# Two-layer hybrid encoder trunk on one core: order of the queues, norms inside the output projections, gain row spread by TensorE

## The chip, the cores and the metric

The kernel runs as one launch on 1 core of one Trainium2 chip. The metric is the device time of that core in microseconds (us). Of the kernel before, 3 runs are given: median 3146.25 us (3145.14 to 3149.17).

## The reference

512 tokens of width 1024 pass through two layers, all in float32:

```
x = x + even_mix(rms_norm(x))   # conformer convolution (GLU, causal conv 31, LayerNorm, swish)
                                # beside chunked gated linear attention; one output projection
x = x + peer_ffn(rms_norm(x))
x = x + fox_mix(rms_norm(x))    # forgetting attention: QK norm, forget gates, causal softmax, out projection
x = x + peer_ffn(rms_norm(x))

def peer_ffn(h):                # 8 heads, 128 x 128 product keys, 16 of 16384 experts for each head
    q = h @ wq; s1, s2 = scores against two key tables
    top 16 of each, 256 sums, top 16 of these -> experts, gates = softmax
    act = gelu(h . u[expert]);  out = sum(gates * act * v[expert])
```

## The kernel before

Tokens are in four blocks of 128 rows. `self.xb[b]` holds block b of x ([128, 1024]); `hT` is the normalised x, turned so that the width lies on the partitions, and kept as two parts, `hhi` (rounded to fp32r) and `hlo` (the rest). A product is made of three fp32r matmuls: hi by hi, hi by lo, lo by hi (`mm3`, L75 to L79). Weights come through `weight` (L54): a DMA from the SP queue into `raw` (4 buffers of 512 KB), then ScalarE makes `whi` (L50) and VectorE, or GpSimd where `eng` says so, makes `wlo` (L51), with 3 buffers each.

The stages follow one another: `mix_even`, `peer(0)`, `mix_odd`, `peer(1)`.

Each stage begins with a norm (`rms_h`, L87 to L125). For a block, `scale` takes the sum of squares (ScalarE, L104, into a tile `sq` of its own), makes the root (VectorE L105, GpSimd L106) and writes `xs` = x times root times gain (VectorE L107); `flip` turns `xs` by 8 transposes (TensorE L114) and splits the result into hi (ScalarE L116) and lo (VectorE L117). The gain row `grow` is loaded by a DMA that repeats it on all 128 partitions (L85, 512 KB).

A mixing part ends in `out_proj` (L194): for each half c of the output columns four accumulators, one for each block, are filled over 4 weight tiles (`kp`, each two k-steps, so 24 matmuls of 512 columns for four blocks). In the second half the last three weight tiles run block after block, in the order 1, 2, 3, 0, and each block is added to x (L199). The norm of the PEER stage is traced behind that.

In the attention (`mix_odd_body`) the scores run in units: (head pair, head, block of queries). `unit()` does the `logits` of one unit (L639 to L648), the `flip` of the unit three back (L658 to L663) and, after a head's last, `values` (L671). `project(hp, w, unit)` calls `unit()` after every second k-step, 56 times in all; 12 calls are left and run ahead of `out_proj` (L704). PSUM tiles come from a pool of 6 banks (`bank`, L72) and one of 2.

`peer_body` (L814): queries and routing of 8 heads, four `u_step`s behind each head (L938). A `u_step` (L842) multiplies one of 128 tiles of u by the tokens of blocks 1 to 3: 24 matmuls of 384 columns, then Gelu. Beside the steps after routing the gate table G is built (`gate4`, L891) and stored to DRAM, and block 0's own expert rows are gathered on the GpSimd queue. When the last gate is built, the pool of the v stage is opened and `fetch` (L950) is called for the first eight places (L1007): it loads parts of G (`gc`, 1.5 MB, L957) and stored activations (`at`, L960) on the SP queue. In the v stage `prepare(n)` (L962) loads a v tile, multiplies `gc` by the activations (L971) and splits the product into `wh` and `wl`; `v_sweep` (L1022) does 18 matmuls of 512 columns for each n.

Each engine and each DMA queue works through a fixed list in order. The program is traced in Python, and a planner puts each engine's instructions in order by times that it simulates, the earlier traced first where several could go. `tc.issue_after(ins)` holds what is traced within it behind `ins` on the same engine or queue.

## Time and profile before

| | us |
|---|---|
| median of 3 runs | 3146.25 |
| profiled execution, own time | 3148.14 |
| its span, first to last instruction | 3146.3 |
| TensorE busy | 3080.9 (98% of the span) |
| VectorE busy | 2406.8 (76%) |
| ScalarE busy | 1437.2 (46%) |
| GpSimd busy | 1155.1 (37%) |

The span is what one core's engines need; the time has the start and end around it. Matmuls overlap one another, so busy time of TensorE is no measure of work, but its idle time and the clock that it was granted can be read place by place.

### The profile page before, as it was taken

To read this page: it belongs to the slowest core of one execution; us is meant where nothing else is said; L and a number is where in the kernel's file an instruction comes from. 1 tells how busy PE (TensorE), PEld (TensorE's weight loads), DVE (VectorE), ACT (ScalarE), POOL (GpSimd) and SP (SyncE) were. 2 spreads that over 40 slices of the span, in tenths; PEclk is the share of its full clock that TensorE was granted. 3 is DMA by queue.
4 is the path that set the end of the run, shared out by engine and by line. 5 is a ranking of instruction groups with operands and counts; after the bars stand their busy time and mean duration, and the time that the engine had idled before them with its cause. 6 is when DMAs were issued, how large, how long until landed. Compare 5 with 4: busy or idle time off the path is not lost.

```text
span 3146.3 us, 45733 instructions
## 1 busy us (share of the span) xinstructions
PE 3080.9 (98%) x15932; PEld 2696.8 (86%) x15932; DVE 2406.8 (76%) x4936; ACT 1437.2 (46%) x2258; POOL 1155.1 (37%) x800
## 2 busy tenths in 40 slices
PE   8999999999999999999999999999999999999999
PEld 6668999999999888877766679999999998888787
DVE  6765998888885888888535548998888867888786
ACT  4343334666664333333356633336666643333332
POOL 1220122996773332332100000227976752233330
PEclk9999999999999999999999999999999999999999
DMA  4113445999998999999421124448999997999996
GB/s 155 54 34 125 137 140 168 358 351 347 339 323 292 310 350 372 352 350 356 148 81 41 41 77 132 137 144 313 375 340 339 339 322 260 354 367 346 355 349 233
DMA packets 334202, 787.16 MB, mean 250 GB/s; under 512 B 26745, under 2 KB 181770, under 8 KB 327826
## 3 DMA queue, kind: packets, MB, share of 16 engines
q1 hardware_dynamic: 260242, 515.76, 47.0%
q0 software_dynamic: 73728, 268.47, 24.1%
q8 instruction: 125, 2.05, 0.3%
q14 instruction: 107, 0.88, 0.1%
HBM read 687.59 MB, written 96.47 MB: 249 GB/s over the span
## 4 chain that ended last, share of the span: by engine, by line
PE 90%; DVE 3%; DMA 2%; issue 1%; ACT 1%; SPq 1%; POOL 1%; DVEq 0%; ACTq 0%; POOLq 0%
PE acc L1027 33%; PE pu L79 10%; PE pu L78 10%; PE pu L77 10%; PE bank L77 5%; PE bank L79 5%; PE bank L78 5%; PE bank L911 5%; PE po L671 1%; PE pc L284 1%; PE bank L639 1%; PE bank L935 1%; DVE wlo L51 1%; SPq L960 1%; POOL gr L861 1%
## 5 line engine op out<-in xcount | busy, mean ns | idle before, releaser
L50 ACT ACTIVATE whi<-raw 128x1024 fp32r<-128x1024 f32 x604 | 636.9, 1057 | 829.5 <-PE pu L78 471.6
L51 DVE TENSOR_TENSOR wlo<-raw,whi 128x1024 fp32r<-128x1024 f32 x565 | 692.1, 1226 | 183.1 <-ACT whi L50 156.3
L77 PE MATMUL pu<-hhi,whi 128*128 128x384 f32 x2048 | 702.0, 343 | 9.6 <-ACT whi L50 8.7
L79 PE MATMUL pu<-hhi,wlo 128*128 128x384 f32 x2048 | 691.0, 338 | 2.2 <-DVE wlo L51 2.2
L78 PE MATMUL pu<-hlo,whi 128*128 128x384 f32 x2048 | 689.2, 337 | 0.0
L872 POOL DMA_INDIRECT gr<-in_vF_dram,ids x256 | 317.7, 1241 | 717.7 <-DVE x L874 658.7
L1027 PE MATMUL acc<-wlo,wh 128*128 128x512 f32 x1536 | 472.7, 389 | 0.0
L1027 PE MATMUL acc<-whi,wl 128*128 128x512 f32 x1536 | 472.5, 389 | 0.0
L1027 PE MATMUL acc<-whi,wh 128*128 128x512 f32 x1536 | 436.5, 390 | 9.3 <-ACT whi L50 9.3
L861 POOL DMA_INDIRECT gr<-in_uN_dram,ids x256 | 352.5, 1377 | 237.6 <-DVE dots L863 140.7
L50 ACT ACTIVATE wh<-gc 128x384 fp32r<-128x384 f32 x256 | 134.4, 525 | 645.7 <-PE acc L1027 638.0
L77 PEld LDWEIGHTS pu<-hhi,whi 128*128 128x128 f32 x2048 | 388.3, 190 | 12.1 <-ACT whi L50 9.3
L79 PEld LDWEIGHTS pu<-hhi,wlo 128*128 128x128 f32 x2048 | 387.3, 189 | 4.0 <-DVE wlo L51 3.9
L78 PEld LDWEIGHTS pu<-hlo,whi 128*128 128x128 f32 x2048 | 388.1, 190 | 1.9 <-DVE hlo L117 0.6
L1027 PEld LDWEIGHTS acc<-whi,wh 128*128 128x128 f32 x1536 | 287.6, 188 | 72.1 <-ACT whi L50 12.6
L1027 PEld LDWEIGHTS acc<-wlo,wh 128*128 128x128 f32 x1536 | 288.3, 188 | 60.0
L1027 PEld LDWEIGHTS acc<-whi,wl 128*128 128x128 f32 x1536 | 288.3, 188 | 59.8
L901 POOL TENSOR_SCALAR a<-cst,sT 128x128 f32<-128x128 f32 x192 | 330.6, 1722 | 13.2 <-PE bank L911 4.9
L874 DVE SCALAR_TENSOR_TENSOR x<-gr,dots,x 128x1024 f32<-128x1024 f32 x256 | 327.4, 1279 | 0.3
L863 DVE CUSTOM_DVE_ANT_0 gr<-gr,h 128x1024 f32<-128x1024 f32 x256 | 307.9, 1221 | 23.8 <-DMA gr<-in_uN_dram,ids 23.7
L51 DVE TENSOR_TENSOR wl<-gc,wh 128x384 fp32r<-128x384 f32 x256 | 142.7, 558 | 179.4 <-ACT wh L50 170.0
L51 POOL TENSOR_TENSOR wlo<-raw,whi 128x1024 fp32r<-128x1024 f32 x39 | 99.0, 2540 | 398.5 <-ACT whi L50 390.5
(248 smaller groups left out, 4242.3 us busy)
## 6 DMA issues: line engine op xcount, KB each, us to landing
raw<-in_uT_dram SPq DMA_DIRECT2D x256, 512.0 KB
raw<-in_vF_dram SPq DMA_DIRECT2D x256, 512.0 KB
G<-big SPq DMA_DIRECT2D x48, 1024.0 KB
gc<-G SPq DMA_DIRECT2D x32, 1536.0 KB
aside<-xact SPq DMA_DIRECT2D x208, 192.0 KB
at<-aside SPq DMA_DIRECT2D x104, 384.0 KB
raw<-in_w_in_dram SPq DMA_DIRECT2D x32, 512.0 KB
raw<-in_wq_dram SPq DMA_DIRECT2D x32, 512.0 KB
```

Source lines behind the costliest of these rows:

```text
L50: first = self.nc.scalar.activation(hi, raw, AF.Copy)
L51: self.last_lo = (eng or self.nc.vector).tensor_tensor(lo, raw, hi.bitcast(F32), op=ALU.subtract)
L77: mm(out, lh, rh, start=first, stop=False)
L78: mm(out, lh, rl, start=False, stop=False)
L79: return mm(out, ll, rh, start=False, stop=last)
L861: nc.gpsimd.indirect_dma_start(out=r, out_offset=None, in_=uN, in_offset=bass.IndirectOffsetOnAxis(ap=ids[:, s:s + 1], axis=0))
L863: return lambda: nc.vector.tensor_tensor_reduce(r, r, h0, 1.0, 0.0, ALU.mult, ALU.add, accum_out=dots[:, s:s + 1])
L872: nc.gpsimd.indirect_dma_start(out=r, out_offset=None, in_=vF, in_offset=bass.IndirectOffsetOnAxis(ap=ids[:, s:s + 1], axis=0))
L874: return lambda: nc.vector.scalar_tensor_tensor(self.x0, r, dots[:, s:s + 1], self.x0, op0=ALU.mult, op1=ALU.add)
L901: (nc.vector if t else nc.gpsimd).tensor_scalar(a1[:, t], self.iota, e1[:, t:t + 1], gate[:, t:t + 1], op0=ALU.is_equal, op1=ALU.mult)
L911: nc.tensor.matmul(p[:, t], a2[:, t], a1[:, t], start=True, stop=True)
L1027: nc.tensor.matmul(acc[b][c], wt[:, s], vt[:, c], start=(n == 0 and wt is wh and vt is vh), stop=(n == NE1 - 1 and wt is wl))
```

## The change

Seven edits, with names that the diff shows:

1. The first gain row is loaded once (4 KB) and spread over 128 partitions by a matmul with a row of ones; then come the loads of x, of four weight tiles (`early`) and of the constants. The table `steps` is loaded and widened in `peer(0)`, by GpSimd.
2. `norm` replaces `rms_h`: its three parts `scale`, `flip`, `close` are called one by one. Sums of squares write into `xs` itself, which has 3 buffers (4 in the first norm).
3. `out_proj` opens the next norm and scales blocks 1, 2 and 3 as they are added (`ends`). `chain` holds the pieces in order on TensorE. In `mix_odd` a new `hT` is there, and the flips of 1, 2 and 3 stand between the pieces of block 0; in `mix_even` they stand behind them, in `peer`.
4. `peer` scales block 0, then one `u_step` is run, then block 0 is flipped; head 0 is followed by three steps and not four.
5. The last 12 units of the attention are called within the first half of `out_proj`, four after each of its weight tiles.
6. The forget gate's projection is traced ahead of the rest of the first half of v.
7. Queue order: `gc` and `at` loads stand behind the newest weight load on SP; `wh` behind `whi` of the same n on ScalarE; the first fetches come 7 steps after the pool is opened (`SETTLE`); the table load for the attention stands behind the last Gelu of the u steps too.

```diff
+SETTLE = 7
     def weight(self, src, shape=None, eng=None, after=None):
-        raw = self.ws.tile([P, D], F32, tag="raw", name="raw", bufs=4)
-        nc.sync.dma_start(raw, src)
+        raw = self.early.pop(0) if self.early else self.raw(src)
...
+            self.last_hi = self.split(raw, hi, lo, eng)
...
+    def norm(self, i, blocks=3):
+        pool = self.tc.tile_pool(name=f"rms{i}", bufs=1, side="right", reuse_waits="tile")
...
-            xs[b] = h0 if b == 0 and h0 is not None else rp.tile([P, D], F32, name="xs", bufs=2)
-            sq = rp.tile([P, D], F32, name="sq")
-            self.last_sq = nc.scalar.activation(sq, self.xb[b], AF.Square, accum_out=ss)
+            xs[b] = rp.tile([P, D], F32, name="xs", bufs=blocks) if dst is None else dst
+            self.last_sq = nc.scalar.activation(xs[b], self.xb[b], AF.Square, accum_out=ss)
...
+    def chain(self):
+        last = []
+        def run(f, *args):
+            if last:
+                with self.tc.issue_after(last.pop().ins):
+                    last.append(f(*args))
+            else:
+                last.append(f(*args))
+            return last[0]
+        return run
...
             if done:
                 ws = load(order[end:])
-                for b in BLOCKS:
-                    sweep(ws, [b])
-                    done(b, acc[b])
+                done([lambda b, w=w: sweep([w], [b]) for w in ws], acc)
...
+        def ends(sweeps, acc):
+            run = self.chain()
+            def finish(b):
+                add(1, b, acc[b])
+                if b:
+                    nc.sync.dma_start(self.kept[b - 1], self.xb[b])
+                    scale(b)
+            for b in DB:
+                for f in sweeps:
+                    run(f, b)
+                finish(b)
+            for n, f in enumerate(sweeps):
+                if hT and n == 0:
+                    run(flip, 1, hT)
+                    run(flip, 2, hT)
+                if hT and n == 2:
+                    run(flip, 3, hT)
+                run(f, 0)
+            finish(0)
+            self.run = run
+        for b, acc in enumerate(self.proj_nat(w[0], yT, order=order, between=between)):
             add(0, b, acc)
+        if middle:
+            middle()
+        self.keep()
+        self.next_norm = scale, flip, _ = self.norm(i)
+        self.proj_nat(w[1], yT, order=order, done=ends)
...
     def mix_even(self):
+        with tc.tile_pool(name="gain", bufs=1, side="right", reuse_waits="tile") as gp:
+            g = gp.tile([1, D], F32, name="g")
+            row = gp.tile([1, P], F32, name="row")
+            nc.vector.memset(row, 1.0)
+            nc.sync.dma_start(g, A["gains"][0:1])
+            for c in range(2):
+                p = self.bank()
+                nc.tensor.matmul(p, row, g[:, c * 512:(c + 1) * 512], start=True, stop=True)
+                nc.scalar.activation(self.grow[:, c * 512:(c + 1) * 512], p, AF.Copy)
+        for b in range(1, NB):
+            nc.sync.dma_start(self.xb[b], A["x"][b * P:(b + 1) * P])
+        self.early = [self.raw(A["w_in0"][i]) for i in (0, 4, 3, 7)]
...
-                        dg = sb.tile([P, P], F32, name="dg", bufs=4)
+                        dg = sb.tile([P, P], F32, name="dg", bufs=3)
...
     def mix_odd(self):
-        with tc.issue_after(self.last_gelu.ins):
+        with tc.issue_after(self.last_gelu.ins), tc.issue_after(self.last_act.ins):
             nc.scalar.preload_act_table_set("natural_log_exp_and_others")
...
-            vproj(0, rest())
             fh, fl = self.small_weight(sc, A["w_fz"], 16, "wf")
             for k in range(KD):
                 self.mm3(pf, fh[:, k], fl[:, k], hT[0][:, k], hT[1][:, k], k == 0, k == KD - 1)
+            vproj(0, rest())
...
-            for _ in range(8 + AHEAD + 1):
-                unit()
-            self.out_proj(A["w_out1"], self.rows(oT))
+            self.hT = self.new_hT()
+            self.out_proj(A["w_out1"], self.rows(oT), 3, hT=self.hT, between=lambda: [unit() for _ in range(4)],
+                          middle=lambda: pool.__exit__(None, None, None))
...
     def peer(self, L):
+                nc.sync.dma_start(self.stf, A["steps"])
+                for w in range(2):
+                    nc.gpsimd.tensor_copy(self.steps[:, w], self.stf[:, w, :, None].to_broadcast([P, TOPK, TOPK]))
+            scale, flip, close = self.next_norm
+            hT = self.hT
+            if not hT:
+                hT = self.new_hT()
+                for b in DB:
+                    self.run(flip, b, hT)
+            scale(0, h0)
+            def last():
+                self.run(flip, 0, hT)
+                close()
+                self.close_x()
...
     def peer_body(self, L, hT, h0, last, sp, sb):
-        nu = 0
+        self.run(lambda: u_step(0)[1])
+        nu = 1
+        last()
...
-                for i in range(WQU):
+                for i in range(WQU - (hd == 0)):
...
-                nc.sync.dma_start(gcs[m], G[:, :, e * TG:(e + EC) * TG].rearrange("g p n -> p g n"))
+                with tc.issue_after(self.last_raw.ins):
+                    nc.sync.dma_start(gcs[m], G[:, :, e * TG:(e + EC) * TG].rearrange("g p n -> p g n"))
...
-            self.split(w, *[t.rearrange("p (g t) -> p g t", t=TG) for t in (wh, wl)])
+            with tc.issue_after(hi.ins):
+                self.split(w, *[t.rearrange("p (g t) -> p g t", t=TG) for t in (wh, wl)])
...
                 vb = vpool.__enter__()
+                opened = nu
+            if vb and nu == opened + SETTLE:
                 for n in range(-AHEAD, AHEAD):
                     fetch(n)
```

## Rows read from the trace of the kernel before

**Rows 1.** The page's busy time, share of the span and instructions by engine.

```profile
PE 3080.9 (98%) x15932; PEld 2696.8 (86%) x15932; DVE 2406.8 (76%) x4936; ACT 1437.2 (46%) x2258; POOL 1155.1 (37%) x800
```

**Rows 2.** Waits of TensorE: waiter, releaser; us in all, times, longest.

```profile
PE bank L114 <- DVE xs L107: 11.0, 2, 10.4
...
PE acc L1027 <- ACT whi L50: 9.3, 8, 1.2
...
PE pu L77 <- ACT whi L50: 8.7, 2, 4.4
```

**Rows 3.** Windows: stretch, us, busy PE PEld DVE ACT POOL (count), PEclk, DMA share, GB/s.

```profile
19.70:23.10 3.40, 1.64 (x5) 0.62 (x4) 3.35 (x6) 2.10 (x4) 0.84 (x2) 1.00 0.80 230
23.10:29.95 6.85, 5.84 (x14) 4.22 (x15) 3.19 (x4) 0.00 (x0) 0.00 (x0) 0.50 0.54 181
268.00:279.00 11.00, 7.96 (x50) 6.41 (x48) 8.77 (x12) 8.00 (x14) 1.58 (x3) 1.00 0.23 86
279.10:286.00 6.90, 5.29 (x15) 4.76 (x16) 4.45 (x7) 0.93 (x2) 0.00 (x0) 0.51 0.68 243
996.00:1006.20 10.20, 5.72 (x21) 4.90 (x20) 4.40 (x7) 4.54 (x7) 1.95 (x1) 0.67 0.81 298
1006.20:1012.00 5.80, 5.80 (x35) 5.80 (x34) 3.48 (x4) 3.74 (x5) 0.00 (x0) 1.00 0.85 278
1587.00:1597.00 10.00, 7.88 (x24) 5.98 (x23) 3.49 (x5) 2.21 (x4) 0.00 (x0) 0.66 0.18 58
1798.00:1812.00 14.00, 10.38 (x32) 6.08 (x32) 6.34 (x17) 5.70 (x13) 0.00 (x0) 0.63 0.01 3
1867.40:1883.40 16.00, 10.62 (x43) 8.60 (x42) 14.18 (x20) 8.54 (x13) 3.21 (x4) 0.68 0.31 100
2592.00:2603.60 11.60, 6.91 (x23) 6.08 (x22) 5.38 (x8) 4.27 (x6) 1.69 (x1) 0.71 0.82 305
```

**Rows 4.** SP queue ahead of the v stage of layer 0.

```profile
970.75 6.08 SPq L957 DMA_DIRECT2D gc<-G  x2
976.88 13.76 SPq L960 DMA_DIRECT2D at<-aside  x3
990.69 0.94 SPq L58 DMA_DIRECT2D raw<-in_uT_dram  x2
```

**Rows 5.** ScalarE and TensorE, timeline in the v stage of layer 0.

```profile
1351.04 0.52 ACT L50 ACTIVATE wh<-gc 128x384 fp32r<-128x384 f32 x1 [3.56 <-PE acc L1027]
...
1352.56 1.67 PE L1027 MATMUL acc<-whi,wh 128*128 128x512 f32 x6 [1.16 <-ACT whi L50]
```

**Rows 6.** First norm and what it is compared with: TensorE and VectorE, timeline.

```profile
14.11 5.73 PE L114 MATMUL bank<-cst,xs 128*128 128x128 f32 x24 [1.75 <-DVE ss L105]
...
274.00 1.09 PE L114 MATMUL bank<-cst,xs 128*128 128x128 f32 x8 [0.57 <-DVE xs L107]
...
18.34 2.21 DVE L51 TENSOR_TENSOR wgl<-wgr,wgh 128x128 fp32r<-128x128 f32 x1
...
23.89 1.27 DVE L117 TENSOR_TENSOR hlo<-bank,hhi 128x512 fp32r<-128x512 f32 x2
```

**Rows 7.** Groups by line: matmuls of plain float32, 512 columns, x4 in two records each.

```profile
L495 PE MATMUL pn<-sq,cst 128*128 128x512 f32 x8 | 4.1, 619 | 0.0
```

**Rows 8.** Tail of the attention: TensorE and ScalarE, timeline.

```profile
1801.65 0.76 PE L639 MATMUL bank<-ka,qa 66*128 66x128 f32 x2 [3.62 <-issue]
...
1802.89 0.37 ACT L645 ACTIVATE pr<-bank,nm 128x128 f32<-128x128 f32 x1 [2.11 <-DVE nm L642]
```

**Rows 9.** Norm of the second PEER: TensorE and VectorE, timeline.

```profile
1868.41 0.15 DVE L105 TENSOR_SCALAR ss<-ss 128x1 f32<-128x1 f32 x1
...
1870.57 5.69 PE L114 MATMUL bank<-cst,xs 128*128 128x128 f32 x24 [2.79 <-DVE ss L105]
```

**Rows 10.** Norm of the first PEER, block 0 on VectorE.

```profile
271.72 0.69 DVE L199 TENSOR_TENSOR x<-x,bank 128x512 f32<-128x512 f32 x1 [1.84 <-PE bank L79]
...
275.27 1.28 DVE L107 SCALAR_TENSOR_TENSOR h<-x,rs,grow 128x1024 f32<-128x1024 f32 x1
```

More of the change, by code (lines that the diff above doesn't have):

```diff
@@ L52, in split, with raw @@
         return first
+    def raw(self, src):
+        raw = self.ws.tile([P, D], F32, tag="raw", name="raw", bufs=4)
+        self.last_raw = self.nc.sync.dma_start(raw, src)
+        return raw
     def weight(self, src, shape=None, eng=None, after=None):
         nc = self.nc
[L57 to L58 removed]
+        raw = self.early.pop(0) if self.early else self.raw(src)
         hi = self.ws.tile([P, D], F32R, tag="whi", name="whi", bufs=3)
@@ L62, in weight @@
             with self.tc.issue_after(after.ins):
-                self.split(raw, hi, lo, eng)
+                self.last_hi = self.split(raw, hi, lo, eng)
         else:
-            self.split(raw, hi, lo, eng)
+            self.last_hi = self.split(raw, hi, lo, eng)
         if shape:
@@ L117, in flip, with close, keep @@
                 nc.vector.tensor_tensor(lo, p, hi.bitcast(F32), op=ALU.subtract)
-        scale(order[0])
-        for n, b in enumerate(order):
-            if n + 1 < NB:
-                scale(order[n + 1])
-            flip(b)
-            if after:
-                after(b)
+            return mm
+        def close():
+            pool.__exit__(None, None, None)
+            if i + 1 < 4:
+                self.load_gain(i + 1)
+        return scale, flip, close
+    def keep(self):
+        self.kept = self.dp.tile([len(DB), P, D], F32, name="kept")
+    def chain(self):
[8 more added lines that the diff above has]
+        return run
     def new_hT(self):
@@ L164, in sweep @@
                         s = slice(b * P, (b + 1) * P)
-                        self.mm3(acc[b], hT[0][k][:, s], hT[1][k][:, s], wh[:, a], wl[:, a],
-                                 kp == order[0] and a == 0, kp == order[-1] and a == 1)
+                        mm = self.mm3(acc[b], hT[0][k][:, s], hT[1][k][:, s], wh[:, a], wl[:, a],
+                                      kp == order[0] and a == 0, kp == order[-1] and a == 1)
+            return mm
         first = load(order[:lead])
@@ L192, in small_weight, with out_proj @@
         return hi, lo
-    def out_proj(self, w, yT, order=range(4)):
+    def out_proj(self, w, yT, i, order=range(4), hT=None, between=None, middle=None):
         nc = self.nc
@@ L199, in add @@
             nc.vector.tensor_tensor(xa, xa, acc, op=ALU.add)
-        for b, acc in enumerate(self.proj_nat(w[0], yT, order=order)):
-            add(0, b, acc)
-        self.proj_nat(w[1], yT, order=order, done=lambda b, acc: add(1, b, acc))
+        def ends(sweeps, acc):
[19 more added lines that the diff above has]
+        for b, acc in enumerate(self.proj_nat(w[0], yT, order=order, between=between)):
+            add(0, b, acc)
+        if middle:
[3 more added lines that the diff above has]
+        self.proj_nat(w[1], yT, order=order, done=ends)
     def log_sigmoid(self, sp, z, shape, dst):
@@ L230, in mix_even @@
         hT = self.new_hT()
-        with tc.tile_pool(name="m0c", bufs=1) as sc:
-            self.rms_h(0, hT)
+        self.grow = self.np.tile([P, D], F32, name="grow", bufs=1)
+        with tc.tile_pool(name="gain", bufs=1, side="right", reuse_waits="tile") as gp:
[10 more added lines that the diff above has]
+        self.early = [self.raw(A["w_in0"][i]) for i in (0, 4, 3, 7)]
+        with tc.tile_pool(name="m0c", bufs=1) as sc:
+            nc.sync.dma_start(self.cst[:, P:], A["consts"][:, P:])
+            scale, flip, close = self.norm(0, NB)
+            for b in range(NB):
+                scale(b)
+                flip(b, hT)
+            close()
             self.mix_even_body(hT, sc)
@@ L548, in mix_odd @@
             start, rest = self.nat_parts(A["w_v1"][0], self.rows(hT), 2, eng=nc.gpsimd)
-            self.rms_h(2, hT, after=start)
+            scale, flip, close = self.norm(2)
+            for b in range(NB):
+                scale(b)
+                flip(b, hT)
+                start(b)
+            close()
             self.mix_odd_body(hT, sc, rest)
@@ L554, in mix_odd_body @@
         self.t2 = 4
-        with tc.tile_pool(name="m1", bufs=1) as sp, tc.tile_pool(name="m1b", bufs=2) as sb:
+        with tc.tile_pool(name="m1", bufs=1) as sp:
+            pool = tc.tile_pool(name="m1b", bufs=2)
+            sb = pool.__enter__()
             qkg = sc.tile([P, 2], F32, name="qkg")
@@ L1079, in build @@
             self.steps = cp.tile([P, 2, TOPK, TOPK], BF16, name="steps")
-            stf = cp.tile([P, 2, TOPK], F32, name="stf")
-            nc.sync.dma_start(stf, A["steps"])
-            for w in range(2):
-                nc.scalar.activation(self.steps[:, w], stf[:, w, :, None].to_broadcast([P, TOPK, TOPK]), AF.Copy)
-            self.load_gain(first)
-            for b in range(1, NB):
-                nc.sync.dma_start(self.xb[b], A["x"][b * P:(b + 1) * P])
-            nc.sync.dma_start(cst[:, P:], A["consts"][:, P:])
+            self.stf = cp.tile([P, 2, TOPK], F32, name="stf")
+            self.cst, self.early = cst, []
             for i, f in enumerate((self.mix_even, lambda: self.peer(0), self.mix_odd, lambda: self.peer(1))):
```

44 lines of the change are left out of this document (17 added, 27 removed).

## The prediction

> **What bounds the kernel now.** I read the page's busy times first. TensorE is busy for 3080.9 us of a span of 3146.3 us [rows 1]; its own weight loads apart, no engine is over 77%. So a gain can come from three things alone: TensorE's 65 us of idle time, the stretches in which it was granted half its clock, or fewer matmuls. The change removes no matmul of the reference's work. The second view is the list of TensorE's waits: the longest are the first norm (10.4 us until the first transpose), eight waits of the v stages for a `whi`, 9.3 us in all, and two of the u steps for a `whi` [rows 2]. The third is a row of windows around each place where matmuls start late. Each shows the same pattern: some us idle and, around it, a mean granted clock of 0.63 to 0.71, against 1.00 in a quiet stretch [rows 3]. [...] What a window loses is its idle time plus (1 - clock) of its busy time. By name:
>
> - ahead of the v stages: 996 to 1006.2 loses 4.5 + 0.33 x 5.7 = 6.4 us, 2592 to 2603.6 loses 4.7 + 0.29 x 6.9 = 6.7 us [rows 3], 13.1 together;
> - in the v stages: the eight waits, 9.3 us [rows 2];
> - norm of the first PEER: 3.0 us idle in 268 to 279 and 1.6 + 0.49 x 5.3 = 4.2 us up to 286, 7.2 in all [rows 3];
> - forget gate: 2.1 + 0.34 x 7.9 = 4.8 us [rows 3];
> - tail of the attention: 3.6 + 0.37 x 10.4 = 7.5 us [rows 3];
> - norm of the second PEER: 5.4 + 0.32 x 10.6 = 8.8 us [rows 3];
> - start: TensorE idles 10.4 us [rows 2], and from 23.1 to 29.95 loses another 1.0 + 0.5 x 5.8 = 3.9 us [rows 3].
>
> All but the start come to 50.7 us. The change touches each of these places, and that is what the sum is made of.
>
> **The change part by part.**
>
> *Loads on SP behind the weights (edit 7).* Ahead of the v stage SP issues two `gc` loads of 1.5 MB and three `at` loads in 970.75 to 990.64, and only then the next `raw` for a u step [rows 4]. That `raw` is late, and TensorE stands (the wait of `pu` for `whi` [rows 2]). Held behind the newest weight load, and called 7 steps later, they no longer pass the weights. Cost: the first `gc` now has some four u steps before it is used, 4 x 24 matmuls at 5.8/35 = 0.166 us [rows 3], 16 us; 1.5 MB at the 298 GB/s of this stretch [rows 3] takes 5 us. Behind the waiting `gc` on SP stand only the next weight loads, which have four buffers. I take 12.5 of 13.1; bounds 6 (one layer alone mended) and 13.1.
>
> *`wh` behind `whi` on ScalarE (edit 7).* At 1351.04 ScalarE makes a `wh` that had waited 3.56 us for a free buffer, with the `whi` that TensorE needs behind it in the list; the `whi` follows, and the matmul starts 1.16 us late [rows 5]. One such row stands for eight. With `whi` first the wait goes: 9.3 us, bounds 6 and 9.3. What queues behind a waiting `wh` is then the next n's `whi`, which is not yet needed.
>
> *Forget gate earlier (edit 6).* The 2.1 us idle and the half clock behind it come from the gate's logarithm chain on ScalarE and VectorE with nothing left to multiply. Now 2 weight tiles of v, 48 matmuls, lie behind the gate's projection and hide a chain of such a length. I take 4.0 of 4.8; bounds 0 and 4.8.
>
> *Last 12 units within the projection (edit 5).* Before, TensorE stood 3.62 us ahead of the last head pair's first score and then ran at half clock [rows 8, 3]. Now it has 24 projection matmuls between every four units. What speaks against it is PSUM: four accumulators take four of the six banks, and two are left for scores and transposes. The smallest score block held its bank from 1801.65 to the end of its exponential at 1803.26 [rows 8], 1.6 us, so 12 units pass through two banks in some 12 to 24 us (an estimate: larger blocks hold it up to twice as long). Three weight tiles of 24 matmuls fill some 16 us of that, and the units' own matmuls the rest. It is close, so I take 5.5 of 7.5; bounds -6.5 (a wait of 1 us at each unit, and nothing won) and 7.5.
>
> *Norm of the second PEER (edits 2 to 4).* VectorE did the first `ss` at 1868.41, when all blocks had been added; the transposes waited for it 2.79 us and took 5.69 us for 24 [rows 9], against 1.09 us for 8 at full clock [rows 6]. Now blocks 1 to 3 are scaled one after the other while TensorE is still on block 3 or 0, and are flipped between block 0's pieces. Left is block 0: from its add at 271.72 to its scaled rows at 276.55 it took 4.8 us in layer 0 [rows 10]; one `u_step` of 24 x 0.166 = 4.0 us covers most, and then 8 transposes, a copy and a subtraction stand ahead of the queries, some 1.5 us (an estimate, from 1.09 and 0.64 [rows 6]). Left over: 2.5 us. I take 6.3 of 8.8; bounds 0 and 8.8. Each kept store stands on SP among the next weights, as before.
>
> *Norm of the first PEER.* The same, but its `hT` becomes free only after the last matmul of the projection, so 24 transposes (3 x 1.09 [rows 6]), six copies and six subtractions of 0.64 us [rows 6] come then, one behind the other. About 0.5 us more stays than above, 3.0, and I take 4.2 of 7.2; bounds 0 and 7.2. The two copies for `steps` on GpSimd fall where it is busy for 1.6 of 11 us [rows 3] and cost nothing; they would cost where the squares' roots stand behind them, under 1 us each.
>
> *Start (edits 1 and 2).* The 512 KB gain row goes; at the 230 GB/s of this stretch [rows 3] x lands 2.2 us sooner, and a 2.21 us split of the gate's weights that stood among the last subtractions on VectorE [rows 6] need not stand there. The last subtraction ended at 25.16 [rows 6]. Against it: two matmuls in plain float32 take 4.1/4 = 1 us each [rows 7], twice that at half clock, 4 us, and a copy; so the gain row is hardly sooner than before. They run while TensorE idles, but if the first squares wait for them (the ones and the row lie where `xs` will be), block 0 is 2 us later. I take 5; bounds -2 and 8.3 (2.2 + 2.2 + 3.9).
>
> `dg` with three buffers costs nothing while ScalarE keeps ahead of the taps; its bound is 3 us.
>
> [...] Did the clock come up for transposes alone? From 14.11 on, 24 took 5.73 us, 0.24 each, against 1.09/8 = 0.14 [rows 6], so they ran at half clock; in 19.70 to 23.10 the clock is 1.00 [rows 3], with no other matmul run before it. [...]
>
> **Sum.** 12.5 + 9.3 + 4.0 + 5.5 + 6.3 + 4.2 + 5.0 = 46.8 us. The profiled execution took 3148.14 us, so 3101.3; it lies 1.9 us above the median of the runs, so 3099 us.
>
> **Rivals.**
>
> 1. *Only the queues and the gate hold* (12.5 + 9.3 + 4.0 = 25.8): the norms' and the tail's pieces are put in order by simulated times, and each place gets a new wait as long as the old. For: the long waits of now arose in such an order too. Against: pieces are now fixed on TensorE by `chain`. 3120 us.
> 2. *Banks*: the units starve on two banks and lose 6.5 instead of winning 5.5. For: 1.6 us and more a bank [rows 8]. Against: the projection's matmuls can fill in. 3111 us.
> 3. *Slower*: `gc` loads come late in the v stages, since they stand behind weight loads that wait for buffers, on a queue that moves about 300 GB/s. A late one stops TensorE for up to the 5 us of its transfer. There are 15 behind the first in each v stage; from 10 late ones of 30 on (50 us) all is lost, and with 15 the time is 3099 + 75 = 3174 us. For: SP works in order. Against: a `gc` is asked for eight places ahead, 8 x 18 matmuls.
> 4. *Clock stays low behind transposes*: then the 24 matmuls of each first u step and the first 15 projection matmuls run at half clock: 4.0 + 4.0 + 2.9 = 11 us lost, 3110 us.
> 5. *No change*: every mended place gives back what it took, 3146 us; it needs the queue pins to bind nothing, which [rows 4, 5] speak against.
>
> **How the numbers follow.** Forecast 0.54 (its own range 3089 to 3109), better than that 0.03, rival 1 0.15, rival 2 0.13, rival 4 0.05, no change 0.04, slower 0.06. A measurement of this kernel tells about 0.2%, 6.3 us, from no change. Faster by more: 0.54 + 0.03 + 0.15 + 0.13 + 0.05 = 0.90; same 0.04; slower 0.06. All upper bounds at once give 13.1 + 9.3 + 4.8 + 7.5 + 8.8 + 7.2 + 8.3 = 59, 3087 us; a little below it for places not counted, 3083, is the low end. The high end takes in rival 1 with some us about it, 3124.
>
> **What would show it.** Right: TensorE's waits for `whi` in `acc` and `pu` gone; no window at half clock ahead of the v stages or behind 1590; no `ss` of block 1 behind block 0's add; the last units lie among projection matmuls at full clock; the first projection runs in an unbroken row before 22 us. Wrong: new waits of TensorE on banks in the output projection of the attention, a VectorE product waiting for `gc` or `at`, or a first transpose later than the 10.4 us of now. The prediction as a whole fails if TensorE's idle time stays above 45 us.

## The result and the profile after

The changed kernel takes 3114.43 us (3113.76 to 3115.09, 4 runs) against 3145.69 us: a ratio of 0.9899 with the 95% interval [0.9882, 0.9916], some 31 us less. The forecast was 47 us less; 3114 lies inside its stated range (3083 to 3124), but above the 3089 to 3109 of the case that it held most likely, and nearest to the price of its second rival (3111). The profiled execution took 3114.21 us, its span 3112.4.

The page's busy time, share of the span and instructions by engine, kernel after [rows 1]:

```profile
PE 3066.9 (99%) x15936; PEld 2684.7 (86%) x15936; DVE 2403.7 (77%) x4937; ACT 1386.0 (45%) x2224; POOL 1096.8 (35%) x802
```

TensorE's idle time fell from 65.4 to 45.5 us, and its busy time by 14 us although it has four records more: so the same work was done in shorter matmuls, at a higher clock (a mean of 0.997 where before had 0.990) or closer behind one another. ScalarE lost 34 instructions and 51 us, which no term of the forecast had (34 table loads of 1.283 us make up 43.6 of it, see e6); that leads to the main finding.

TensorE's waits, kernel after (waiter, releaser; us in all, times, longest) [rows 2]:

```profile
PE bank L114 <- DVE xs L107: 8.8, 3, 5.1
...
PE bank L286 <- DMA g<-in_gains_dram: 4.7, 1, 4.7
PE bank L114 <- DVE ss L105: 3.9, 1, 3.9
PE pu L82 <- ACT hhi L116: 3.4, 1, 3.4
PE bank L82 <- ACT hhi L116: 3.1, 2, 1.7
```

The waits for `whi` in the v stages and u steps are gone. What leads now is norms: the wait of 5.1 us is the norm that opens layer 1, which the prediction never priced. The last row holds the queries of the two PEER stages, which wait 1.7 and 1.4 us for block 0's copies.

Windows at the places of [rows 3] and at that norm, kernel after (stretch, us, busy PE PEld DVE ACT POOL, PEclk, DMA share, GB/s):

```profile
268.00:276.80 8.80, 8.09 (x49) 6.86 (x47) 6.79 (x9) 4.96 (x8) 0.57 (x2) 1.00 0.31 107
276.80:288.20 11.40, 6.42 (x20) 6.16 (x21) 5.57 (x8) 3.10 (x6) 0.55 (x1) 0.70 0.51 155
990.00:1010.02 20.02, 20.02 (x118) 20.02 (x117) 10.75 (x17) 7.24 (x13) 3.26 (x2) 1.00 1.05 353
1536.00:1548.00 12.00, 6.51 (x24) 4.95 (x24) 8.71 (x11) 7.94 (x14) 9.58 (x7) 0.72 0.42 132
1578.70:1588.70 10.00, 10.00 (x45) 7.23 (x44) 1.94 (x4) 2.69 (x4) 0.00 (x0) 1.00 0.32 107
1800.00:1830.00 30.00, 27.19 (x120) 17.12 (x119) 13.94 (x32) 8.85 (x21) 0.00 (x0) 1.00 0.12 36
1846.00:1862.00 16.00, 15.26 (x87) 12.70 (x85) 11.93 (x17) 10.09 (x17) 1.65 (x3) 1.00 0.31 109
2563.00:2581.04 18.04, 18.04 (x106) 18.04 (x105) 8.38 (x12) 6.36 (x10) 3.26 (x2) 1.00 1.04 357
```

Clean now: ahead of both v stages, the forget gate (1578.7) and, but for the 1.4 us ahead of its queries, the second PEER's norm (1846). Not clean: the first PEER's norm (276.8), the norm of layer 1 (1536) and the units inside the projection (1800, 2.8 us idle).

To see where the time went I cut each trace at the starts of the same matmuls. In the names, `pn` belongs to the gated attention, `pu` to the u steps and `acc` to the v stage; the 200th is counted from 0. The columns are differences from before in us (negative is shorter), each from one profiled run; the runs e3 to e12 are described below:

| stretch up to | before, us | after | e11 | e6 | e3 | e5 | e12 |
|---|---|---|---|---|---|---|---|
| first convolution matmul | 77.5 | -1.5 | -1.8 | -0.8 | -1.5 | -1.5 | -0.4 |
| last convolution matmul | 116.6 | +4.7 | 0.0 | 0.0 | +4.7 | +4.7 | 0.0 |
| last `pn` of the gated part | 32.8 | -1.7 | 0.0 | 0.0 | -1.7 | -1.7 | +0.1 |
| 200th `pu` of layer 0 | 128.2 | +3.3 | -0.4 | -0.3 | -3.4 | +3.3 | -1.8 |
| last gate transpose, layer 0 | 608.5 | -0.3 | +2.3 | +3.0 | +2.0 | +0.4 | -1.2 |
| last `acc`, layer 0 | 581.0 | -13.0 | -13.0 | 0.0 | -13.0 | -13.0 | -13.0 |
| 200th `pu` of layer 1 | 409.2 | -14.4 | -16.2 | -14.1 | -16.2 | -18.9 | -18.6 |
| last gate transpose, layer 1 | 605.5 | +2.7 | +1.9 | -0.3 | +4.2 | +2.2 | +0.9 |
| last `acc`, layer 1 | 581.8 | -13.8 | -13.8 | +0.3 | -13.8 | -13.8 | -13.8 |

The two rows that end at a gate transpose vary by up to 4.2 us either way, once (in e1) by 7.9, in kernels that differ in nothing there; the others repeat within 1.4 us between two runs of one kernel, most of them to hundredths.

### The profile page after: what moved, and what is told of

The parts are those of the page before. It is cut to its first block, busy times and chain, and to the rows that moved or that the text cites. A ratio compares the mean times of both kernels' runs of the same rounds, so it can differ in the third digit from the quotient of the medians.

```text
span 3112.4 us, 45713 instructions
## 1 busy us (share of the span) xinstructions
PE 3066.9 (99%) x15936; PEld 2684.7 (86%) x15936; DVE 2403.7 (77%) x4937; ACT 1386.0 (45%) x2224; POOL 1096.8 (35%) x802
## 4 chain that ended last, share of the span: by engine, by line
PE 82%; DVE 3%; issue 2%; DMA 2%; POOL 1%; ACT 0%; DVEq 0%; POOLq 0%; ACTq 0%
PE acc L1114 33%; PE pu L83 10%; PE pu L84 10%; PE pu L82 10%; PE bank L989 4%; PE bank L82 4%; PE bank L84 4%; PE bank L83 4%; DMA gr<-in_uN_dram,ids 2%; PE po L744 1%; PE bank L712 1%; PE bank L1017 1%; DVE gr L941 1%; DVE wlo L52 1%; PE bank L731 1%
## 5 line engine op out<-in xcount | busy, mean ns | idle before, releaser
L950 POOL DMA_INDIRECT gr<-in_vF_dram,ids x256 | 279.1, 1090 | 718.7 <-DVE x L952 694.3
L1114 PE MATMUL acc<-wlo,wh 128*128 128x512 f32 x1536 | 439.5, 389 | 0.0
L1114 PE MATMUL acc<-whi,wl 128*128 128x512 f32 x1536 | 438.4, 389 | 0.0
L941 DVE CUSTOM_DVE_ANT_0 gr<-gr,h 128x1024 f32<-128x1024 f32 x256 | 307.9, 1221 | 23.8 <-DMA gr<-in_uN_dram,ids 23.7
L979 POOL TENSOR_SCALAR a<-cst,sT 128x128 f32<-128x128 f32 x192 | 317.2, 1653 | 15.4 <-PE bank L989 6.7
L976 DVE TENSOR_TENSOR a<-cst,sT 128x512 f32<-128x512 f32 x192 | 133.1, 693 | 127.8 <-PE bank L989 116.7
L82 PE MATMUL bank<-hhi,whi 128*128 128x512 f32 x512 | 210.9, 413 | 3.1 <-ACT hhi L116 3.1
```

The source lines that it names most:

```text
L82: mm(out, lh, rh, start=first, stop=False)
L941: return lambda: nc.vector.tensor_tensor_reduce(r, r, h0, 1.0, 0.0, ALU.mult, ALU.add, accum_out=dots[:, s:s + 1])
L950: nc.gpsimd.indirect_dma_start(out=r, out_offset=None, in_=vF, in_offset=bass.IndirectOffsetOnAxis(ap=ids[:, s:s + 1], axis=0))
L976: nc.vector.tensor_tensor(a2, self.iota[:, None, :].to_broadcast([P, 4, P]), e2[:, :, None].to_broadcast([P, 4, P]), op=ALU.is_equal)
L979: (nc.vector if t else nc.gpsimd).tensor_scalar(a1[:, t], self.iota, e1[:, t:t + 1], gate[:, t:t + 1], op0=ALU.is_equal, op1=ALU.mult)
L1114: nc.tensor.matmul(acc[b][c], wt[:, s], vt[:, c], start=(n == 0 and wt is wh and vt is vh), stop=(n == NE1 - 1 and wt is wl))
```

## The experiments

Medians, and ratios to the kernel before on the same chip:

| run | what it is | us | ratio |
|---|---|---|---|
| e1, e11 | before + edit 7 | 3107.17, 3106.80 | 0.9875 [0.9859, 0.9892], 0.9878 [0.9862, 0.9895] |
| e2 | before + `wh` behind `whi` | 3129.66 | 0.9949 [0.9932, 0.9966] |
| e6 | before + table load held | 3135.86 | 0.9962 [0.9948, 0.9976] |
| e4 | before + three `dg` | 3148.83 | one run |
| e10 | after again | 3112.71 | 0.9893 [0.9876, 0.9909] |
| e3 | after + order at the first PEER's norm | 3108.42 | 0.9878 [0.9861, 0.9894] |
| e5 | after - edit 5 | 3108.25 | 0.9873 [0.9856, 0.9889] |
| e7 | after + gain row's pool moved | 3114.82 | 0.9893 [0.9877, 0.9910] |
| e8 | after + e3 + e5 | 3104.84 | 0.9866 [0.9849, 0.9882] |
| e9 | e8 + GpSimd's splits held | 3106.51 | 0.9877 [0.9861, 0.9894] |
| e12 | e8 + four `dg` | 3099.91 | 0.9847 [0.9833, 0.9862] |

**e1 and e11, edit 7 alone.** The three last hunks of the change's diff, its line for the table load in `mix_odd`, and its `last_hi`, `last_raw` and `last_act`, on the kernel before.

> The kernel before with edit 7 alone (queue order, SETTLE, place of the table load). Theory A (the pins do the work by themselves): the v stages' eight waits of 1.16 us and the two waits of 4.2 and 4.5 us ahead of them go, with the half clock behind these; by the marks of the two traces this is 13.0 us in layer 0 and 13.9 us in layer 1, so 3119 us, 0.9915 of before. Theory B (the gain there needs the other edits too, since they shift what the planner orders): under 15 us, 3131 us or more.

> The kernel before with the order of the queues alone (edit 7), again, beside the kernel after. Theory A (edit 7 carries the whole gain, and edits 1 to 6 together lose some microseconds): 3106 to 3110 us, 4 to 9 us under the kernel after. Theory B (the whole change is better than its queues, the first comparison was chance): 3112 us or more, at or above the kernel after.

3107.17 and 3106.80 us; beside e11 the kernel after took 3112.71. The queues' edit alone wins 38 to 39 us, more than the whole change, so edits 1 to 6 together cost about 6 us, though the two intervals overlap. The traces say the same: summed over the stretches of the table that repeat, after is 36.4 us shorter than before, and the two kernels with edit 7 alone 42.2 and 45.2. For e1 theory A was expected at 3119 us; what it left out, some 12 us, is about what the table load of e6 wins. The v stages are shorter by 13.0 and 13.8 us in every kernel with edit 7.

The SP queue ahead of the v stage, kernel after [rows 4]:

```profile
975.38 0.38 SPq L1040 DMA_DIRECT2D gc<-G  x1
979.11 4.49 SPq L57 DMA_DIRECT2D raw<-in_uT_dram  x2
```

One `gc` stands between weights here, not two `gc` and three `at` ahead of them. ScalarE and TensorE in the v stage, kernel after [rows 5]:

```profile
1340.91 1.06 ACT L51 ACTIVATE whi<-raw 128x1024 fp32r<-128x1024 f32 x1 [2.61 <-issue]
1341.88 0.51 ACT L51 ACTIVATE wh<-gc 128x384 fp32r<-128x384 f32 x1
...
1344.74 1.52 PE L1114 MATMUL acc<-whi,wh 128*128 128x512 f32 x6
```

`whi` comes first, and the matmul has no wait.

**e2, one pin of edit 7.**

```diff
...
-            self.split(w, *[...])
+            with tc.issue_after(hi.ins):
+                self.split(w, *[...])
```

> The kernel before with only `wh` held behind `whi` on ScalarE. Theory A: the eight late matmuls go and nothing else, 8 x (1.546 - 0.227) = 10.6 us, 3135 us; the two waits ahead of the v stages stay, 4.2 and 4.5 us. Theory B (the order on ScalarE is a symptom, and the weights themselves come late): the eight waits turn up at another instruction, no gain, 3146 us.

The v stages are shorter by 6.2 and 6.3 us, 12.4 in all (forecast 9.3). So the loads' part of the 26.9 of all of edit 7 is 14.4, by difference (forecast 12.5). The idle time understated the eight waits: from start to start each cost 1.32 us, not 1.16 (10.6 in all; the other 1.8 I did not place). The attention, which e2 doesn't touch, is 7.2 us shorter here, and 3.3 in e4: the order written out for it comes out differently, and a difference of some us there proves nothing by itself. It is the likely reason why e2 came out 5 us under the 3135 us expected.

**e6, the other pin of edit 7, the table load.**

```diff
...
-        with tc.issue_after(self.last_gelu.ins):
+        with tc.issue_after(self.last_gelu.ins), tc.issue_after(self.last_act.ins):
             nc.scalar.preload_act_table_set("natural_log_exp_and_others")
```

> The kernel before, with one part alone: the attention's table load held behind the last Gelu of the u steps of layer 0 (the last line of edit 7). Theory A: the table loads of ScalarE fall from 47 to 13; the waits of TensorE at the forget gate and ahead of the last head pair (3.6 us and half clock behind it) shrink or go, and the attention is shorter by 10 to 14 us, 3131 to 3136 us beside 3145.3 of the kernel before. Theory B (the loads of 1.28 us lie beside TensorE's work and cost nothing, the gains at the gate and at the tail are edits 5 and 6): 3143 to 3147 us, with the 3.6 us wait still there.

`last_act` names the last Gelu of the u steps; `last_gelu` in this run is that of block 0's own experts alone. 3135.86 us, and the attention 14.1 us shorter. ScalarE's timeline of the kernel before shows why:

```profile
1004.16 1.28 ACT L545 ACT_TABLE_LOAD   x1
...
1007.24 1.28 ACT L853 ACT_TABLE_LOAD   x1
...
1796.86 1.28 ACT L223 ACT_TABLE_LOAD   x1
...
1798.85 1.28 ACT L224 ACT_TABLE_LOAD   x1
```

The load for logarithm and exponential came at 1004.16 (L545), and a last Gelu of the u steps (L853) brought a load of its own at 1007.24. From there the logarithm and the exponential of the forget gate and, but for the first logarithm, all of the QK norm came with a table load each. Groups of table loads by line, kernel before (count | us, mean ns | idle):

```profile
L224 ACT ACT_TABLE_LOAD x16 | 20.5, 1283 | 0.3
L223 ACT ACT_TABLE_LOAD x15 | 19.2, 1283 | 0.3
```

In e6 and after both lines are gone, and of 47 loads 13 are left. With the load held behind that Gelu, one load (L545 in e6, L612 in after) serves the whole attention; without, a logarithm and the exponential behind it took two. Each load took 1.283 us, with at most 0.02 us of idle time ahead of it in the attention.

In e6 the forget gate and the tail of the attention, where before lost 4.8 and 7.5 us [rows 3], without edits 5 and 6:

```profile
1586.77:1596.77 10.00, 9.97 (x45) 7.16 (x44) 3.59 (x7) 3.28 (x5) 0.00 (x0) 1.00 0.35 107
1785.06:1799.06 14.00, 13.59 (x68) 8.06 (x67) 11.73 (x33) 8.60 (x22) 0.00 (x0) 1.00 0.13 39
```

Both are clean. In e2, which keeps the 47 loads, the same windows read:

```profile
1576.80:1586.80 10.00, 7.88 (x35) 5.43 (x34) 3.41 (x6) 3.32 (x6) 0.00 (x0) 1.00 0.18 57
1783.40:1797.40 14.00, 10.39 (x33) 6.03 (x32) 6.34 (x17) 5.85 (x13) 0.00 (x0) 0.63 0.02 6
```

TensorE waits 2.12 us at the gate and 3.61 at the tail there, as in before. So the gate's wait and the whole loss of the tail belong to this pin, to which the prediction gave no price. The half clock behind the gate's wait doesn't: e2 has the wait and a clock of 1.00, where before had 0.66. Cut at the same matmuls, e6's 14.1 us are 2.1 for the gate's wait, 3.0 for the half clock behind it (0.50 from 1591 to 1595 in before), 8.0 for the tail and 1.0 elsewhere. The 2.1 and the 8.0, some 10 us, were won by no kernel that keeps the loads (e2, e4); the 3.0 comes off in e2 too.

**e5, edit 5 taken back.**

```diff
...
+            for _ in range(8 + AHEAD + 1):
+                unit()
             self.hT = self.new_hT()
-            self.out_proj(..., between=lambda: [unit() for _ in range(4)], middle=...)
+            self.out_proj(..., middle=...)
```

> The kernel after, with one part taken back: the last 12 units of the attention run ahead of the output projection again (edit 5 undone); everything else as changed. Theory A (the units inside the projection starve on two free banks, the prediction's second rival; the gain seen at this place comes from the tables that are no longer loaded): the time from the first matmul of the output projection to the 200th of the u steps of layer 1, plus the tail ahead of it, shrinks by 6 to 9 us, 3105 to 3109 us beside the 3114.4 of the kernel after; TensorE's waits of 0.4 to 0.8 us for PT copies between 1800 and 1830 us vanish, and no wait of 3.6 us comes back at the tail. Theory B (the units are hidden inside the projection, the lost microseconds there lie with the second norm): no change or slower, 3113 to 3121 us, with the 3.6 us wait and half clock back ahead of the last head pair.

3108.25 us beside 3114.82 for e7, which is the kernel after in all but the start: 6.6 us less, though the two intervals overlap. The traces put 4.5 of it into the attention's stretch (-18.9 against -14.4), where 6 to 9 were expected. TensorE inside the projection, kernel after:

```profile
1806.64 1.12 PE L712 MATMUL bank<-ka,qa 66*128 66x512 f32 x2 [0.69 <-ACT PT L734]
...
1810.81 0.50 PE L82 MATMUL bank<-whi,ohi 128*128 128x512 f32 x1 [0.43 <-ACT ohi L748]
...
1817.95 1.12 PE L712 MATMUL bank<-ka,qa 66*128 66x512 f32 x2 [0.69 <-ACT PT L734]
```

A score block waits until the copy of the block before has emptied a bank. In e5 the longest stop in the last 30 us of the units is 0.6 us, not on a bank, and PE is busy for 28.97 of 30:

```profile
1780.00:1810.00 30.00, 28.97 (x133) 17.76 (x132) 16.97 (x45) 13.15 (x31) 0.00 (x0) 1.00 0.06 19
```

Moving the units costs time: the second rival, at about 4.5 us where it was priced at 6.5. No wait of 3.6 us came back; the table load stays behind the last Gelu in e5.

**e3, the first PEER's norm.**

```diff
...
-            scale(0, h0)
+            with tc.issue_after(self.last_copy.ins):
+                scale(0, h0)
```

`last_copy` names the last `hhi` copy of `flip`; the line stands in `peer`, so it acts in both PEER norms.

> The kernel after, with block 0's squares in both PEER norms held behind the copies of the flips of blocks 1 to 3 on ScalarE, and so the first query weights too. Theory A (in the first PEER norm TensorE stood 3.4 us since the last two copies came behind block 0's squares and two weights on ScalarE): the first u step starts about 276.5 instead of 279.5 and the wait of 3.4 us falls under 1 us; 3 to 6 us are won, 3109 to 3111 us. Theory B (the flips themselves come too late, because hT is free only after the last projection matmul, and VectorE's subtractions bound it): the wait for `hlo` takes the place of that for `hhi`, under 1 us is won, 3114 us.

ScalarE and TensorE, kernel after:

```profile
273.94 2.06 ACT L116 ACTIVATE hhi<-bank 128x512 fp32r<-128x512 f32 x4 [1.71 <-PE bank L114]
275.87 1.08 ACT L104 ACTIVATE h<-x 128x1024 f32<-128x1024 f32 x1
...
276.91 2.02 ACT L51 ACTIVATE whi<-raw 128x1024 fp32r<-128x1024 f32 x2
278.80 1.10 ACT L116 ACTIVATE hhi<-bank 128x512 fp32r<-128x512 f32 x2
...
273.31 2.78 PE L114 MATMUL bank<-cst,xs 128*128 128x128 f32 x24
279.47 0.44 PE L82 MATMUL pu<-hhi,whi 128*128 128x384 f32 x1 [3.38 <-ACT hhi L116]
282.23 0.69 PE L83 MATMUL pu<-hlo,whi 128*128 128x384 f32 x1 [2.32 <-DVE hlo L117]
```

The last two `hhi` copies stand behind block 0's square and two weight copies, 3 us. In e3:

```profile
273.97 3.05 ACT L116 ACTIVATE hhi<-bank 128x512 fp32r<-128x512 f32 x6 [1.71 <-PE bank L114]
...
273.34 2.78 PE L114 MATMUL bank<-cst,xs 128*128 128x128 f32 x24
276.58 0.44 PE L82 MATMUL pu<-hhi,whi 128*128 128x384 f32 x1 [0.46 <-ACT hhi L116]
```

The stretch is 6.7 us shorter than after, 3.4 shorter than before: theory A. The time is 3108.42 us, 4 to 6 us under the two runs of after, with overlapping intervals.

**e4, three `dg` buffers.** `bufs=4` to `bufs=3` on the kernel before.

> The kernel before with three `dg` buffers and not four. Theory A (the third buffer's loss breaks the runs of convolution matmuls, and each change between plain float32 and fp32r costs): the last convolution matmul starts 3 to 5 us later than in the kernel before (194.17), with about twice the 30 changes of kind between 70 and 205 us; 3148 us. Theory B (the new order of the first norm did it): 30 changes or so, last convolution matmul within 1 us of 194.2; 3146 us.

The last convolution matmul stands 3.1 us later than in before, and 4.7 us later behind the first one. From the first one to the 200th `pu` of layer 0 e4 needs 2.6 us more than before, and e8 3.0 more than e12. TensorE has no idle time in 77 to 200 us in either kernel; its order differs. Groups in that window, before (x | busy us, mean ns | idle):

```profile
L284 PE MATMUL pc<-upad,dg 128*128 128x512 f32 x84 | 38.9, 596 | 0.0
...
L79 PE MATMUL bank<-hhi,wlo 128*128 128x512 f32 x64 | 25.1, 392 | 0.0
```

and after, to whose rows e4's are alike:

```profile
L350 PE MATMUL pc<-upad,dg 128*128 128x512 f32 x83 | 41.7, 603 | 0.0
...
L84 PE MATMUL bank<-hhi,wlo 128*128 128x512 f32 x62 | 25.5, 412 | 0.0
```

From 70 to 205 us TensorE changes from a tap (plain float32) to another matmul or back 30 times in before and e12, 64 times in after, e4 and e8. So the buffer count sets the order, and the longer time goes with it; that the changes themselves cost the time is theory A, and no run separates them from the rest of the order.

**e7, the start.** `side="right"` taken from the gain row's pool.

> The kernel after, with the gain row's pool on the other side of the memory, so that the first squares no longer share addresses with the ones and the row and need not wait for the two f32 matmuls. Theory A (the start won 1.5 instead of 5 us because the squares stood behind these matmuls and their copies): the first square starts near 4.5 us instead of 9.02, the first convolution matmuls come 2 to 4 us sooner, 3110 to 3112.5 us beside 3114.4. Theory B (the gain row itself, its two matmuls at half clock and copies, sets the start: the scaled block needs it whenever the squares are made): first scaled block no sooner than 12 us, 3113.5 to 3115.5 us.

The first square came at 4.29 us, but the second half of the gain row was now copied behind two more squares, at 10.55, and the first scaled block began at 11.23 (11.03 in after). Nothing won: theory B, whose bound of 12 us was 0.8 high. The start, kernel after [rows 6]:

```profile
4.74 3.75 PE L286 MATMUL bank<-g,row 1*128 1x512 f32 x4 [4.74 <-DMA g<-in_gains_dram]
12.37 3.98 PE L114 MATMUL bank<-cst,xs 128*128 128x128 f32 x16 [3.89 <-DVE ss L105]
...
21.95 1.94 PE L114 MATMUL bank<-cst,xs 128*128 128x128 f32 x8 [2.13 <-DVE xs L107]
23.73 1.22 PE L82 MATMUL bank<-hhi,whi 128*128 128x512 f32 x2
```

**e8, both repairs (e3 and e5).**

> The kernel after with two edits together: the units ahead of the output projection again, and head 0's query weights held behind the copies of the flipped blocks 1 to 3 on ScalarE, as in the run on the norm of the first PEER. If the two losses are separate (theory A): 6 us of the one and 6 to 9 us of the other, 3099 to 3103 us. If they share a cause (theory B, both are one wait of VectorE and ScalarE moved about): no better than the better of the two, 3106 to 3109 us.

3104.84 us: lower than either, with intervals that overlap theirs, and short of the full sum; it lies between the two theories. In the traces the units' saving is there whole (388.7 us in the attention's stretch against 393.0 in e3), the norm's in part (5.1 of 6.7 us against after).

**e9, GpSimd's splits behind the roots.** On top of e8, the subtractions of the first weights of each layer are issued behind the last `rs` of the blocks already scaled; in layer 1 the scaling of blocks 0 to 2 is also traced ahead of these weights.

> The kernel with both repairs (units ahead of the projection again, head 0's query weights behind the copies of the flips), and a third: GpSimd's weight subtractions at the start and at the first norm of layer 1 are held behind the roots of the norm's blocks. Theory A (the norm of layer 1 lost 5.1 us of TensorE and half clock behind it, because the roots stood behind two weight subtractions of 4.7 us, and VectorE scaled three blocks in 5.8 us beside the third): the idle time at the first transpose of layer 1 falls from 5.1 to 2.5 us or less, the roots of the start's last block come 2 us sooner; 4 to 8 us less than the kernel with the two repairs, about 3097 to 3101 us where that is 3104.8. Theory B (the scaled blocks themselves, 1.3 us each on VectorE behind the last addition, set the wait, and the subtractions that are moved come late instead): within 2 us of it, 3103 to 3107 us, with a new wait of TensorE on wlo.

The norm of layer 1, GpSimd and VectorE, kernel after:

```profile
1535.18 4.69 POOL L52 TENSOR_TENSOR wlo<-raw,whi 128x1024 fp32r<-128x1024 f32 x2 [54.82 <-ACT whi L51]
1539.83 2.30 POOL L106 TENSOR_TENSOR rs<-ss,sc 128x1 f32<-128x1 f32 x3
...
1540.43 5.79 DVE L107 SCALAR_TENSOR_TENSOR xs<-x,rs,grow 128x1024 f32<-128x1024 f32 x3 [0.68 <-POOL rs L106]
```

and in e9:

```profile
1537.51 8.68 POOL L54 TENSOR_TENSOR wlo<-raw,whi 128x1024 fp32r<-128x1024 f32 x3
...
1537.07 4.58 DVE L114 SCALAR_TENSOR_TENSOR xs<-x,rs,grow 128x1024 f32<-128x1024 f32 x2 [0.61 <-POOL rs L113]
```

The first wait fell from 5.1 to 3.2 us, less than expected, but VectorE's scaling and GpSimd's subtractions still run side by side and stretch: the third block takes 3.38 us, as it took 3.39 in after, where the first of e9 takes 1.28, and the three subtractions take 8.68. TensorE's matmuls of 512 columns start 0.43 us apart until the pace changes at 1547.8, and 0.23 apart from there; the mean clock of 1532 to 1548 is 0.68. That is 14.6 us behind the end of the last `acc` matmul, where it was 10.8 in after (a clock of 0.50 from 1541 to 1547). At the start block 3's root came 2 us sooner, as expected, but the first convolution matmul came 1.5 us later than in e8. 3106.51 us says that nothing is won: theory B in its result, with small waits on `wlo` (0.25 us), `hhi` and `hlo` in place of the one that it named.

**e12, the best version.** Four `dg` again, and the convolution's pool closed where the norm's is opened, as the change itself does in layer 1.

> The kernel with both repairs (units ahead of the projection, head 0's query weights behind the copies of the flips) and dg with four buffers again, for which the convolution's pool is closed between the two halves of the first output projection, where the norm's pool is opened. Theory A (three buffers cost the 3 us by which the convolutions ended later): the last convolution matmul stands 3 us sooner in the stage, about 194.5 us where the kernel with the two repairs had 197.9, and the time is 3 us less, 3100 to 3103 us. Theory B (the later end has to do with the order of the first norm, not with dg): the last convolution matmul at 197 to 198 us, 3103 to 3106 us. Against both, closing the pool there may give the norm's first squares a wait for the convolution's last buffers: the first u step more than 82 us behind the last convolution matmul, where it was 79.2.

3099.91 us, ratio 0.9847 [0.9833, 0.9862], below the intervals of after; that of e8 overlaps it, so what four buffers win over e8 rests on the trace. The last convolution matmul stands at 193.7 us (197.9 in e8): theory A. The cost named against it didn't show: the first u step comes 80.9 us behind it instead of 79.2, and that is the 1.8 us by which the gated part is longer with four buffers (32.9 against 31.1).

e10 was the kernel after again, for e9 and e11:

> The kernel after, unchanged, on the chip of the other two runs, so that they can be compared: 3112 to 3117 us by every theory.

## Why the prediction was right, step by step

The direction held, and the queues' two terms with their mechanism. The sum is near because its errors cancel: forecast 46.8, measured 33.9 in the profiled runs. That is in part luck. The table load, which had no price, won 10 to 14 us; without it the change would have come to some 3124 to 3128 us (an estimate: 3114.4 plus these), at the high end of the range or above it.

| term | forecast | measured | from |
|---|---|---|---|
| loads behind weights | 12.5 | 14.4 | table, e2 |
| `wh` behind `whi` | 9.3 | 12.4 | e2 |
| forget gate earlier; last 12 units | 4.0; 5.5 | won by the table load; the units lose 4.5 | e6, e5 |
| table load behind the last Gelu | no price | 14.1, some 10 of it in no other way | e6, e2 |
| norm of the second PEER | 6.3 | 6.7 | windows |
| norm of the first PEER | 4.2 | -3.3 | table, e3 |
| start | 5.0 | 0.7 to 1.5 | table, e10 |
| three `dg` | 0 (bound 3) | -2.6 to -3.0 | e4, e12 |
| norm of layer 1 | no term | -1.8 | windows |

For the second PEER's norm the window of 16 us lost 8.8 before and 0.7 now, and behind it the queries wait another 1.4 for block 0's copies: 6.7 won, close to the forecast, which had left 1.5 us for these copies. No run tests this part by itself. The norm of layer 1 before, TensorE's timeline and the window:

```profile
1547.23 0.50 PE L77 MATMUL bank<-whi,hhi 128*128 128x512 f32 x1 [1.29 <-ACT hhi L116]
...
1547.00:1559.00 12.00, 8.85 (x39) 7.19 (x40) 8.41 (x9) 3.75 (x8) 6.85 (x5) 0.86 0.51 175
```

It lost 3.15 + 0.14 x 8.85 = 4.4 us there and 1.06 of the first wait ahead of it, 5.5 in all; after, 5.49 + 0.28 x 6.51 = 7.3. In the attention's stretch the terms give 14.1 + 6.7 - 1.8 - 4.5 = 14.5, and the table shows 14.4; part of the 14.1 comes and goes with the order, so the fit is no proof of each term. Over all stages of the table: 1.5 - 3.0 - 3.3 + 26.9 + 14.4 - 2.4 = 34.1, where the 2.4 is the variation of the u steps, and the spans differ by 33.9.

*Queues.* Right, and undersized, since the wait was priced by idle time and not from matmul to matmul. The slower rival didn't come: at 990 to 1010 TensorE is busy for 20.02 of 20.02 us, and no product waits for `gc`.

*Forget gate and tail.* The step that failed is the reading "nothing left to multiply", with the price of 4.0 and 5.5 us on edits 5 and 6. The chain was long because it held table loads, 2 x 1.28 us at the tail, and the row that the prediction quoted [rows 8] lies right behind them. I had looked at TensorE and at the last releaser, and not at what ScalarE did in the gap. The change's third pin was listed and left without a price, and at 10 to 14 us it is worth about as much as the largest term of the sum. What edit 6 does by itself no run tests; without these loads there was nothing left for it to win (the gate's window in e6).

*Last 12 units.* The prediction's bank rival, given 0.13, is what happened at this place, while the total stayed within the stated range because the tables paid. Its estimate of 12 to 24 us for 12 units through two banks doesn't follow from the 1.6 us (12 x 1.6 / 2 = 9.6, up to 19 for larger blocks), which changes nothing here.

*First PEER's norm.* "One behind the other" was costed on TensorE and VectorE alone. On ScalarE block 0's square and two weight copies came between the copies of the flips, and TensorE waited 3.4 and 2.3 us; the clock of 276.8 to 288.2 was 0.70, another 1.9 us (0.30 x 6.42).

*Start.* The gain row was said to be "hardly sooner", which is so; but GpSimd's root of block 3 stood behind a weight subtraction, and VectorE took 3.42 us for one scaled block beside it, where the two before took 1.28 each. The first projection is unbroken from its first matmul at 23.7 us (in before from 24.6), not before 22.

*`dg`.* Priced by ScalarE's lead, while the cost goes with TensorE's order of matmuls.

*Fourth rival.* The u step behind 24 transposes runs at half clock in after (0.50 from 282.23 to 286), behind waits of 3.4 and 2.3 us. In e3, with the same 24 transposes and waits of 0.46 and 1.21, 276.5 to 288 has the clock at 1.00:

```profile
276.50:288.00 11.50, 8.39 (x46) 7.46 (x47) 8.40 (x11) 7.25 (x11) 0.55 (x1) 1.00 0.59 202
```

So transposes alone did not lower it here, and no run shows this rival's condition or its 11 us. That the 24 transposes from 14.11 ran at half clock was the prediction's estimate from their 0.24 us each; the clock recorded there, kernel before, is 1.00:

```profile
14.11:19.84 5.73, 5.66 (x24) 4.70 (x24) 5.28 (x7) 5.73 (x14) 3.88 (x3) 1.00 0.91 316
```

Of the prediction's own signs, waits for `whi` gone, no half clock ahead of the v stages and no `ss` behind block 0's add came true. So did two of its signs of being wrong: TensorE waits on banks inside the attention's output projection, and the first transpose comes at 12.4 us, where it came at 10.4. By its last sign, that it fails if TensorE's idle time stays above 45 us, it failed by half a microsecond (45.5). That sign was ill chosen, as idle time is not all that was lost: 14 us came back as shorter busy time.

Open: why the order of the attention, and with it the half clock behind the gate (0.66 in that window of before, 1.00 in e2), comes out another way in kernels that don't touch it (e2 and e4 moved it by 7.2 and 3.3 us); what the changes of matmul kind cost by themselves; and a start or a norm of layer 1 that wins what was forecast, for which e7 and e9 were no mending.

## What to carry to other kernels

Ask at a stall what every engine did in the gap, table loads included, before pricing it by the engine that waited; count loads by line, and hold a preload behind the last instruction that brings a load of its own (here the last Gelu: 47 loads became 13). Give every edit a price, and test edits alone: here one of seven carried the gain, and the other six together cost a few microseconds as they stood, since what the second PEER's norm won was lost at other places. When work is moved into a place, count its banks and each in-order queue there (ScalarE's copies, GpSimd's roots), since that is where the new waits arose here: 0.69 us on a bank, 3.4 us on copies, 5.1 us on scaled blocks, with their roots behind 4.69 us of weight subtractions.

## What the runs showed of the hardware

- A VectorE scaling of 128x1024 took 1.28 us alone, and 3.42 us beside a GpSimd subtraction of 2.36 (after, at 14.31). The subtraction began 0.01 us sooner and took no longer than others of its kind, of which 39 average 2.51 us. No run shows what makes the scaling wait or slow down.
- With three `dg` buffers TensorE changes 64 times instead of 30 between float32 taps and fp32r matmuls, and the same work takes 2.6 to 3.0 us longer, at a clock of 1.00 and with no idle time in 77 to 200 us. Put down to the changes alone, that is about 0.09 us each (an estimate; the runs don't separate them from the rest of the order).
